# Four sums per SwiGLU on GpSimd instead of VectorE, in a two-layer decoder trunk on one core

## The chip, the cores and the metric

The kernel runs on one core of one Trainium2 chip. A core has TensorE (matrix products, called PE in the profile), VectorE (DVE), ScalarE (ACT), GpSimd (POOL) and SyncE (SP, which here only issues transfers). Each works through its own list of instructions in order, and they wait for each other by semaphores. The metric is the time of one execution in microseconds on the device; the profile is one such execution, recorded by the hardware profiler.

## The reference, cut to what matters

The input is one sequence of 512 tokens with 1024 features, all in float32. Two layers follow each other. Only the SwiGLUs matter here, of which there are four (two a layer):

```python
def swiglu(h, w_gate, w_up, w_down):
    return (jax.nn.silu(h @ w_gate) * (h @ w_up)) @ w_down

for l in range(DEPTH):                      # DEPTH = 2
    x = x + 0.5 * swiglu(rms_norm(x, ffn1_norm[l]), ffn1_wg[l], ffn1_wu[l], ffn1_wd[l])
    ...                                     # sliding-window attention and short convolution
    x = x + 0.5 * swiglu(rms_norm(x, ffn2_norm[l]), ffn2_wg[l], ffn2_wu[l], ffn2_wd[l])
return rms_norm(x, final_norm)
```

The hidden width of a SwiGLU is 2816, which is 22 blocks of 128.

## The kernel before, in words

Every float32 product is made of three faster products: each operand is split into a rounded "high" part (a cast on ScalarE, to `wh` for weights, `...h` for the stream) and the rest, a "low" part (a subtraction on VectorE, to `wl` or `...l`), and high x high, high x low and low x high are added up. The helper `split` (L225) records both. A few weights are split "far" (L229 to L231): ScalarE makes the high part and the negated copy, and a transfer issued by GpSimd adds the weight onto it in memory.

The SwiGLUs 1 to 4 are those of layer 0 (first, second) and layer 1 (first, second). Each begins with one "plain" pair of blocks (`plain`), its down projection (`down`), and then handles the other blocks in larger pairs (`winograd2`), with seven block products instead of eight. For it the stream (features x tokens, already normalized, tiles `hf`, L537) is cut into quarters b11, b12, b21, b22, and a weight of gate and up into a11, a12, a21, a22. From these come four sums of the stream, which are made once in each SwiGLU, for the first such pair, and serve all its pairs: t3 = b12 - b22 (L588), t2 = t3 - b11 (L589), t1 = b11 - b12 in the place of b12 (L591), t4 = t2 + b21 in the place of t2 (L593). Each is one instruction on 128 partitions x 1024 columns. t2 and t3 are made while the plain pair's down projection runs, t1 and t4 in the pair itself.

The products of a pair stand in the table `CHAINS`, in this order, with the weight that each uses: "x" a11 x b11; "w" a12 x b21; "x" s2 x t2; "y" s3 x t3; "x" s1 x t1; "y" a22 x t4; "x" s4 x b22. The s are sums of weights: the loads themselves add two tiles up (a second transfer onto the first, issued by GpSimd, L220), and VectorE adds others (L264, L284). Each product has two halves of the weight (12 matmuls of 512 columns each, 24 in all), and each half has its `wh` and `wl`. Weights are taken two splits ahead of their use, three buffers deep.

The order of the instructions of each engine is fixed when the program is built: a scheduler places each instruction by its own estimate of when its inputs are there. So a change of an instruction's engine moves others too. On the chip nothing overtakes on an engine.

The classes touched are `Norm`, which keeps one `Seven` for the stream's operands of a SwiGLU, and `Seven`, whose `make` builds an operand (the sum, if there is one, and then its split). `Seven` also serves the down projections (`shared`) and the mixer's output (`mix`); those are not touched.

Of the kernel before, what the change touches and what calls it, by code (L numbers as in the profile page):

```python
# [74 lines left out]
def trunk_kernel(  # L75
# [23 lines left out]
    nc = tc.nc  # L99
# [25 lines left out]
    def form(name, dt=F32R, shape=(P, KC // 2, H)):  # L125
        return xpool.tile(list(shape), dt, tag="xf", bufs=14, name=name)
# [97 lines left out]
    def split(hi, lo, raw, eng=nc.vector):  # L224
        return nc.scalar.copy(hi, raw), eng.tensor_sub(lo, raw, f32(hi))  # L225
# [210 lines left out]
    class Norm:  # L436
        def __init__(self, i):
            self.i = i
            self.h = [None] * KC
            self.acc = None  # L440
            self.inv = None
            self.full = []
            self.seven = Seven(self.full, room_g8, f"{i}")
            self.make, self.forms = self.seven.make, self.seven.forms
            self.pairs = {}
            self.begun = set()
            self.order = range(KC)
# [98 lines left out]
    class Seven:  # L546

        def __init__(self, full, room, name, far=()):  # L550

            self.full, self.room, self.name, self.forms = full, room, name, {}
            self.far = far

        def make(self, *names):
            for what in names:
                if what in self.forms:
                    continue
                full = self.full() if callable(self.full) else self.full
                b11, b12, b21, b22 = (  # L560
                    full[j][:, :, t * H : (t + 1) * H] if j < len(full) else None
                    for j in range(2)
                    for t in range(2)
                )
                kc = b11.shape[1]
                if kc == KC // 2:
                    hi, lo = (form(f"f{what}{n}_{self.name}") for n in "hl")
                else:
                    both = form(f"f{what}_{self.name}", shape=(P, 2, kc, H))
                    hi, lo = both[:, 0], both[:, 1]  # L570
                self.forms[what] = (hi, lo)
                if self.room is None:
                    if what == "t2":
                        nc.vector.tensor_sub(b12, b12, b22)
                        nc.vector.tensor_sub(b11, b12, b11)
                    if what == "t1":
                        nc.vector.scalar_tensor_tensor(
                            b12, b11, -1.0, b22, op0=ALU.mult, op1=ALU.subtract
                        )
                    if what == "t4":  # L580
                        nc.vector.tensor_add(b21, b11, b21)
                    places = {"b11": b11, "t2": b11, "t3": b12, "t1": b12, "b21": b21, "t4": b21, "b22": b22}
                    split(hi, lo, places[what])
                    continue
                if what == "t2":
                    self.sums = self.room(self.name)
                    t3, t2 = self.sums
                    nc.vector.tensor_sub(t3, b12, b22)  # L588
                    nc.vector.tensor_sub(t2, t3, b11)  # L589
                if what == "t1":  # L590
                    nc.vector.tensor_sub(b12, b11, b12)  # L591
                if what == "t4":
                    nc.vector.tensor_add(self.sums[1], self.sums[1], b21)  # L593
                src = {"b11": b11, "b21": b21, "b22": b22, "t1": b12}.get(what)
                if src is None:
                    src = self.sums[0 if what == "t3" else 1]
                (split_far if what in self.far else split)(hi, lo, src)
# [1129 lines left out]
```

## Time and profile before

| | |
|---|---|
| time, median of 3 runs | 1632.73 us (1632.26 to 1633.55) |
| the profiled execution | 1633.73 us, span from first to last instruction 1631.9 us |
| granted TensorE clock | 0.999 of full speed |
| TensorE busy | 1619.6 us, 99% of the span |
| VectorE busy | 1369.1 us, 84% |
| ScalarE busy | 1178.7 us, 72% |
| GpSimd busy | 223.5 us, 14% |
| the four sums on VectorE (L588, L589, L591, L593) | about 1.22 us each, 16 in all; in SwiGLU 1 from 44.7 us on, in SwiGLU 4 from 1327.1 us on |

In a timeline each row gives the start (us from the span's start), the length, the engine, the line and the operation, output<-inputs by the program's names, shapes, and how many instructions in a row were merged (x2); in brackets stands how long the engine was idle before and what ended that. In the chain of waits a row has start, length and what ran. A row of transfers says where they were issued, how many, their size and the median time from issue to landing. The length of a transfer's row in a timeline is that of its issue, not of its movement.

### The profile page before, as it was taken

What the parts mean: (1) busy time and instruction counts of PE and PEld (TensorE: products, weight loads), DVE (VectorE), ACT (ScalarE), POOL (GpSimd) and SP (SyncE); (2) the same over time, 40 slices, a digit from 0 to 9 for tenths busy, and PEclk for the clock granted to TensorE, in tenths of its full rate; (3) what the DMA queues carried; (4) which work ended last, traced back from release to release, by engine and by line L of the source; (5) the groups of instructions that cost most, each with busy time, mean ns of one, the idle gap of its engine ahead of it and who ended that gap; (6) DMA issues with size and microseconds to landing.
All of it is one profiled execution on the core that took longest, in us unless ns stands there. A gap on an engine that the chain in (4) does not pass through costs nothing.

```text
span 1631.9 us, 21170 instructions
## 1 busy us (share of the span) xinstructions
PE 1619.6 (99%) x7572; PEld 1348.3 (83%) x7572; DVE 1369.1 (84%) x1779; ACT 1178.7 (72%) x1510; POOL 223.5 (14%) x199
## 2 busy tenths in 40 slices
PE   9999999999999999999999999999999999999998
PEld 6788888888898888888888888888888988888887
DVE  7978798888899877797998777979788998677997
ACT  6667778867766577777865777788586767878665
POOL 1211111001121111111011111110012111111121
PEclk9999999999999999999999999999999999999999
DMA  9899989922497699999966999999136978999992
GB/s 271 194 230 221 215 203 234 251 65 74 125 240 176 175 218 218 214 209 240 229 154 173 227 214 221 199 246 228 52 91 156 227 153 213 222 222 229 230 264 70
DMA packets 307166, 318.12 MB, mean 195 GB/s; under 512 B 125612, under 2 KB 188660, under 8 KB 307060
## 3 DMA queue, kind: packets, MB, share of 16 engines
q1 hardware_dynamic: 265140, 230.63, 49.9%
q0 software_dynamic: 41200, 85.47, 30.9%
q8 instruction: 59, 0.97, 0.2%
q10 hardware_dynamic: 720, 0.66, 0.1%
q14 instruction: 47, 0.39, 0.1%
HBM read 264.29 MB, written 2.10 MB: 163 GB/s over the span
## 4 chain that ended last, share of the span: by engine, by line
PE 89%; DVE 5%; ACT 3%; DMA 1%; issue 1%; SPq 0%; ACTq 0%; DVEq 0%
PE x L823 26%; PE y L823 13%; PE x_s L823 8%; PE w L823 6%; PE acc L311 6%; PE acc L312 6%; PE acc L314 6%; PE y_s L823 5%; PE x_m L808 3%; PE w_s L823 2%; PE y_m L808 1%; DVE wl L225 1%; PE y_e L823 1%; PE acc L685 1%; PE x_e L823 1%
## 5 line engine op out<-in xcount | busy, mean ns | idle before, releaser
L225 DVE TENSOR_TENSOR wl<-raw,wh 128x1024 fp32r<-128x1024 f32 (+1 forms) x493 | 598.4, 1221 | 172.6 <-ACT wh L225 171.7
L225 ACT CAST wh<-raw 128x1024 fp32r<-128x1024 f32 (+1 forms) x493 | 513.1, 1045 | 296.1 <-PE x L823 95.0
L311 PE MATMUL acc<-xh,wh 128*128 128x512 f32 x392 | 153.1, 392 | 0.5 <-ACT wh L225 0.5
L312 PE MATMUL acc<-xl,wh 128*128 128x512 f32 x392 | 153.4, 391 | 0.0
L314 PE MATMUL acc<-xh,wl 128*128 128x512 f32 x384 | 149.8, 390 | 0.0
L220 POOL DMA_DIRECT2D raw<-in_ffn_wu_dram x40 | 50.2, 1263 | 384.6 <-DMA raw<-in_ffn_wu_dram 311.2
L311 PEld LDWEIGHTS acc<-xh,wh 128*128 128x128 f32 x392 | 73.8, 188 | 15.1 <-ACT wh L225 0.6
L312 PEld LDWEIGHTS acc<-xl,wh 128*128 128x128 f32 x392 | 73.7, 188 | 15.0 <-DVE xl L458 0.5
L314 PEld LDWEIGHTS acc<-xh,wl 128*128 128x128 f32 x384 | 72.2, 188 | 15.0
L220 POOL DMA_DIRECT2D raw<-in_ffn_wg_dram x40 | 48.4, 1232 | 201.9 <-DMA raw<-in_ffn_wu_dram 104.7
L220 POOL DMA_DIRECT2D raw<-in_ffn_wd_dram x34 | 41.1, 1218 | 254.5 <-DMA raw<-in_ffn_wd_dram 99.9
L264 DVE TENSOR_TENSOR raw<-raw,raw 128x1024 f32<-128x1024 f32 x58 | 70.5, 1219 | 6.2 <-DMA raw<-in_ffn_wu_dram 4.7
L1085 ACT COPY raw_a<-turned 128x1024 uint16<-128x1024 uint16 x48 | 63.5, 1355 | 0.0
L823 PE MATMUL x<-wl,ft2h 128*128 128x512 f32 x160 | 62.2, 390 | 1.1 <-DVE wl L225 1.1
L823 PE MATMUL w<-wl,fb21h 128*128 128x512 f32 x160 | 62.4, 390 | 0.6 <-DVE wl L225 0.6
L823 PE MATMUL y<-wh,ft4h 128*128 128x512 f32 x160 | 62.4, 390 | 0.1
L823 PE MATMUL w<-wh,fb21h 128*128 128x512 f32 x160 | 62.4, 390 | 0.0
L823 PE MATMUL y<-wh,ft3h 128*128 128x512 f32 x160 | 62.3, 390 | 0.0
L823 PE MATMUL x<-wh,ft2h 128*128 128x512 f32 x160 | 62.3, 389 | 0.0
L823 PE MATMUL x<-wh,ft1h 128*128 128x512 f32 x160 | 62.3, 389 | 0.0
L823 PE MATMUL x<-wh,ft2l 128*128 128x512 f32 x160 | 62.3, 389 | 0.0
L823 PE MATMUL w<-wh,fb21l 128*128 128x512 f32 x160 | 62.3, 389 | 0.0
(506 smaller groups left out, 4544.2 us busy)
## 6 DMA issues: line engine op xcount, KB each, us to landing
raw<-in_ffn_wu_dram SPq DMA_DIRECT2D x127, 512.0 KB, 5.6
raw<-in_ffn_wd_dram SPq DMA_DIRECT2D x105, 512.0 KB, 5.7
raw<-in_ffn_wg_dram SPq DMA_DIRECT2D x86, 512.0 KB, 5.5
raw<-in_ffn_wu_dram POOLq DMA_DIRECT2D x40, 512.0 KB, 9.1
raw<-in_ffn_wg_dram POOLq DMA_DIRECT2D x40, 512.0 KB, 6.3
raw<-in_w_in_dram SPq DMA_DIRECT2D x36, 512.0 KB, 4.1
raw<-in_ffn_wd_dram POOLq DMA_DIRECT2D x34, 512.0 KB, 9.8
raw<-raw POOLq DMA_DIRECT2D x21, 512.0 KB, 8.2
```

Of the source, the lines that this page charges most:

```text
L220: nc.gpsimd.dma_start(out=r, in_=rows_of(*more), accum_op=ALU.add)
L225: return nc.scalar.copy(hi, raw), eng.tensor_sub(lo, raw, f32(hi))
L264: nc.vector.tensor_add(a11, a11, s1)
L311: nc.tensor.matmul(acc, hi[:, k, :], rhs[k][0], start=k == first, stop=False)
L312: nc.tensor.matmul(acc, hi[:, k, :], rhs[k][1], start=False, stop=False)
L314: nc.tensor.matmul(acc, lo[:, k, :], rhs[k][0], start=False, stop=k == last)
L685: nc.tensor.matmul(opening[n], (lo if part == "w" else hi)[:, k, :], xl if part == "x" else xh, start=n not in begun, stop=k == KC - 1 and ...
L808: nc.tensor.matmul(accs[c // 2][:, c % 2, :], w[:, k, cols], x_[:, 2 * h + k, :], start=start and c % 2 == 0 and h + k + i == 0, stop=h + ...
L823: nc.tensor.matmul(accs[u], x_[:, 2 * h + k, tok], w[:, k, :], start=start and h + k + i == 0, stop=h + k == 2 and i == 2, skip_group_chec ...
L1085: nc.scalar.copy(words(raws[self.b][:, c, :]), self.to[:, :, c, :])
```

## The change

`Seven` gets the engine that makes the sums as an argument, VectorE by default; `Norm` passes GpSimd. The splits of the sums stay on ScalarE and VectorE.

```diff
-            self.seven = Seven(self.full, room_g8, f"{i}")
+            self.seven = Seven(self.full, room_g8, f"{i}", adder=nc.gpsimd)
...
-        def __init__(self, full, room, name, far=()):
+        def __init__(self, full, room, name, far=(), adder=nc.vector):
             self.full, self.room, self.name, self.forms = full, room, name, {}
+            self.adder = adder
...
                 if what == "t2":
                     self.sums = self.room(self.name)
                     t3, t2 = self.sums
-                    nc.vector.tensor_sub(t3, b12, b22)
-                    nc.vector.tensor_sub(t2, t3, b11)
+                    self.adder.tensor_sub(t3, b12, b22)
+                    self.adder.tensor_sub(t2, t3, b11)
                 if what == "t1":
-                    nc.vector.tensor_sub(b12, b11, b12)
+                    self.adder.tensor_sub(b12, b11, b12)
                 if what == "t4":
-                    nc.vector.tensor_add(self.sums[1], self.sums[1], b21)
+                    self.adder.tensor_add(self.sums[1], self.sums[1], b21)
```

In the built program this is the order on two of the engines (a weight's half in brackets; "transfer" is one issued by GpSimd):

```
ScalarE, SwiGLU 2 and 4
  before: ft2h, a11(2), ft3h, a12(1), a12(2), ... ft1h, s2(1), s2(2), ... ft4h
  after:  ft2h, ft3h, a11(2), ft1h, a12(1), ft4h, a12(2), ... s2(1), ... s2(2)
ScalarE, SwiGLU 3
  before: ft2h, a11(2), ft3h, a12(1), ft1h, a12(2), ... s2(1), s2(2), ft4h
  after:  ft2h, ft3h, ft1h, a11(2), a12(1), ft4h, a12(2), ... s2(1), ... s2(2)
ScalarE, SwiGLU 1
  before: a12(1), a12(2), ft2h, ... ft3h, ... ft1h, s2(1), s2(2), ... ft4h
  after:  a12(1), ft2h, a12(2), ft3h, ... ft1h, ... s2(1), ft4h, s2(2)

GpSimd after
  SwiGLU 1:    4 transfers of x, t3, 1 of x, t2, 3 of x, t1, t4
  SwiGLU 2, 4: t3, t2, far transfer of a11(1), 2 transfers of s3, t1, t4
  SwiGLU 3:    t3, t2, t1, far transfer of a11(1), 2 transfers of s3, t4
```

The low parts on VectorE follow in the same way: in SwiGLU 1 after: a12(1), ft2l, ft3l, a12(2), ft1l, s2(1), ft4l, s2(2); in SwiGLU 2 and 4 after: a12(1), ft1l, a weight sum, a12(2), a weight sum, s2(1), ft4l.

## The prediction, made before the changed kernel ran

> **What bounds the kernel now.** I read the page's busy line first, then a table of engine time over the four stretches in which a SwiGLU's first pair is computed, then the timelines of TensorE, GpSimd, ScalarE and VectorE and the chain of waits in those stretches.
>
> ```profile
> PE 1619.6 (99%) x7572; PEld 1348.3 (83%) x7572; DVE 1369.1 (84%) x1779; ACT 1178.7 (72%) x1510; POOL 223.5 (14%) x199
> ```
>
> TensorE is busy for 1619.6 of 1631.9 us. An idle GpSimd is no slack by itself: what counts is whether TensorE waits.
>
> ```profile
> 45.00:92.00 47.00, 45.25 (x198) 36.34 (x196) 41.70 (x42) 29.78 (x37) 8.89 (x9) 1.00 0.79 189
> 530.00:558.00 28.00, 28.00 (x125) 23.09 (x124) 26.94 (x28) 18.38 (x22) 1.21 (x1) 1.00 0.54 150
> 853.00:881.00 28.00, 28.00 (x125) 23.17 (x125) 25.85 (x27) 18.09 (x22) 1.84 (x2) 1.00 0.58 170
> 1334.00:1364.00 30.00, 30.00 (x142) 25.03 (x141) 27.02 (x28) 23.22 (x30) 2.90 (x3) 1.00 0.67 177
> ```
>
> The columns are the stretch, its length, then busy time of TensorE, weight load, VectorE, ScalarE and GpSimd. In SwiGLU 2, 3 and 4 TensorE has no idle time to win back. In SwiGLU 1 it idles 47.00 - 45.25 = 1.75 us. So the change can bring at most about 1.75 us, however much it relieves VectorE.
>
> **What is moved, and its price.** Sixteen instructions of VectorE (four in each of four SwiGLUs) go to GpSimd.
>
> ```profile
> 45.80 1.22 DVE L225 TENSOR_TENSOR fb21l<-hf,fb21h 128x1024 fp32r<-128x1024 f32 x1
> 46.93 1.22 DVE L589 TENSOR_TENSOR sums<-sums,hf 128x1024 f32<-128x1024 f32 x1
> ```
>
> Back to back they start 1.13 us apart, so VectorE is relieved of 16 x 1.13 = 18.1 us. No instruction of GpSimd in this trace has 1024 columns; the nearest is its product of 512 columns:
>
> ```profile
> 449.97 1.29 POOL L1658 TENSOR_TENSOR cc<-cc,inv 128x512 f32<-128x512 f32 x1
> ...
> 1601.91 3.52 POOL L1351 TENSOR_TENSOR ytok<-ytok,gain 128x512 f32<-128x512 f32 x2 [12.89 <-ACT ysq L1319]
> ```
>
> ```profile
> 1602.12 2.16 DVE L225 TENSOR_TENSOR wl<-raw,wh 128x1024 fp32r<-128x1024 f32 x1
> ...
> 1604.27 2.25 DVE L225 TENSOR_TENSOR fb22l_e<-raw_a,fb22h_e 128x1024 fp32r<-128x1024 f32 x1
> 1606.44 1.21 DVE L225 TENSOR_TENSOR wl<-raw,wh 128x1024 fp32r<-128x1024 f32 x1
> ```
>
> Alone it takes 1.29 us, so for twice the columns I take 2.6; the ends are 1.3 (the time doesn't grow) and 2 x 1.76 = 3.5 (each of the disturbed pair of 3.52), with a wait of up to 0.9 more. The second fence shows the disturbance: two GpSimd products (own time 2.58) and two VectorE subtractions (2 x 1.13) together fill 1601.91 to 1606.52, that is 4.6 us, the sum 4.84 and not the longer of the two. The engines took turns. So I add to each sum about 0.9 us of waiting wherever VectorE is busy (3.5 in all), and VectorE stands still for 2.6 us in each.
>
> The Trainium skill, page "SBUF — State Buffer", section "Who interferes with whom", says that a VectorE instruction with two SBUF inputs and a GpSimd instruction that reads SBUF exclude each other for their whole length. The trace agrees (4.6 against 4.84); by that rule the change takes up to 16 x 2.6 = 42 us of VectorE's time to save 18, where engines that ran side by side would make the first SwiGLU's loss below about 3 us smaller.
>
> **What is queued behind.** All engines work their queues in order. The built order puts ft1h and ft4h on ScalarE (they cast the third and fourth sum) ahead of casts of the a12 weights that TensorE needs sooner, and puts the sums on GpSimd between transfers. So weights wait for sums that nobody needs yet. One SwiGLU at a time:
>
> *Second SwiGLU.*
>
> ```profile
> 520.91 0.90 POOL L231 DMA_DIRECT2D wl<-raw  x1 [2.55 <-DVE a L225]
> 522.10 1.21 POOL L220 DMA_DIRECT2D raw<-in_ffn_wg_dram  x1 [0.29 <-issue]
> 533.35 1.21 POOL L220 DMA_DIRECT2D raw<-in_ffn_wg_dram  x1 [10.05 <-DMA raw<-in_ffn_wu_dram]
> ```
>
> ```profile
> 530.27 1.06 ACT L225 CAST wh<-raw 128x1024 fp32r<-128x1024 f32 x1 [2.32 <-issue]
> 532.99 1.06 ACT L225 CAST wh<-raw 128x1024 fp32r<-128x1024 f32 x1 [1.66 <-PE x L823]
> ...
> 536.60 1.06 ACT L225 CAST ft1h<-hf 128x1024 fp32r<-128x1024 f32 x1
> ```
>
> ```profile
> 530.41 5.44 PE x L823 x24
> 535.86 5.44 PE w L823 x24
> ```
>
> The two "wh" casts are the halves of a12, used by "w" (a12 x b21) from 535.86 and from 2.72 later. t1 now stands on GpSimd behind the transfer issued at 533.35, which waits for its tile to land: t1 runs 534.56 to 537.2, ft1h to 538.2, a12's first cast to 539.3, that is 3.4 late. Its low part comes 1.2 later on VectorE and is wanted 0.45 after the first product: 0.7 more. t4 ends at 537.2 + 3.5 = 540.7, ft4h at 541.8, the second cast at 542.8; its low part follows low part one, ft1l and a sum on VectorE, to 544, wanted at 535.86 + 4.1 + 2.72 + 0.45 = 543.1: about 0.9 more. **Second: 5.0.** The third far transfer (520.91) now goes out after t3 and t2, some 4 us later; I count that at nothing because it would still land near 531, where its product is due; where it doesn't, it is 1 to 2 us.
>
> *Fourth SwiGLU.* Same order, same steps.
>
> ```profile
> 1337.65 1.21 POOL L220 DMA_DIRECT2D raw<-in_ffn_wg_dram  x1 [9.91 <-DMA raw<-in_ffn_wu_dram]
> ```
>
> ```profile
> 1341.34 5.46 PE w L823 x24
> ```
>
> t1 1338.86 to 1341.5, ft1h 1342.5, cast 1343.6: 2.2 late, and the same 0.7 and 0.9. **Fourth: 3.8.**
>
> *Third SwiGLU.* Here three sums stand ahead of the third far transfer (the low part of the first a11 weight).
>
> ```profile
> 840.40 1.23 POOL L220 DMA_DIRECT2D raw<-in_ffn_wu_dram  x1
> 844.94 0.90 POOL L231 DMA_DIRECT2D wl<-raw  x1 [3.31 <-DVE sums L588]
> ...
> 857.26 1.21 POOL L220 DMA_DIRECT2D raw<-in_ffn_wg_dram  x1 [9.73 <-issue]
> ```
>
> ```profile
> 853.65 5.44 PE x L823 x24
> 859.09 5.44 PE w L823 x24
> ```
>
> ```profile
> wl<-raw POOLq DMA_DIRECT2D x10, 512.0 KB, 7.7
> raw<-in_w_out_dram POOLq DMA_DIRECT2D x8, 512.0 KB, 7.3
> x<-down POOLq DMA_DIRECT2D x8, 256.0 KB, 10.8
> ```
>
> The sums run from 841.6 for 3 x 2.6 and some 1.4 of waiting, to 850.8; the transfer goes out 5.9 us later than at 844.94. At the median of 7.7 us to land that is 858.5, wanted at 853.65 + 0.45: 4.4 late; if it lands faster for having left the crowd, less. I take 3.0. t4 behind the transfer of 857.26 ends near 861.7, ft4h and the second cast near 863.8, wanted near 864.8 after the delay: hidden behind the first wait. **Third: 3.0.**
>
> *First SwiGLU.*
>
> ```profile
> 41.54 6.67 POOL L1247 DMA_DIRECT2D x<-down  x7
> ```
>
> ```profile
> 48.15 1.05 ACT L225 CAST wh<-raw 128x1024 fp32r<-128x1024 f32 x1 [0.88 <-ACT wh L225]
> 49.11 1.05 ACT L225 CAST ft2h<-sums 128x1024 fp32r<-128x1024 f32 x1
> ```
>
> ```profile
> 50.85 0.39 PE L823 MATMUL w<-wh,fb21h 128*128 128x512 f32 x1
> ...
> 58.46 0.50 PE L823 MATMUL x<-wl,ft2h 128*128 128x512 f32 x1 [1.08 <-DVE wl L225]
> ```
>
> VectorE is full here. t3 stands behind four of the transfers (0.95 us each): 45.3 to 48.8; one transfer; t2 49.8 to 53.3; three transfers; t1 56.1 to 59.6; t4 to 63.1. a12's second cast (48.15 before) now follows ft2h: 53.3 + 2.1 = 55.4. Its low part follows ft2l and ft3l on VectorE, with t1 taking 2.6 in between: about 61.3, wanted at 50.85 + 2.72 + 0.45 = 54.0, 7.3 late. The s2 weight follows ft1h and ft1l: about 0.8 more. The 1.1 us that TensorE waited at 58.46 goes. **First: 7.0.**
>
> **The sum.** 7.0 + 5.0 + 3.0 + 3.8 = 18.8 us; TensorE never idles elsewhere enough to give it back. The profiled execution took 1633.73 (span 1631.9 and 1.8 around it), so 1652.5 there; it stood 1.0 above the median 1632.73, so **1651.5** for the median.
>
> **Rivals.** A difference under 0.2% (3.3 us) cannot be told from no change. *Relief wins (not slower):* the sums end before the casts behind them are wanted, and only the 1.75 us are won: 1631. It decides in the second SwiGLU: t1 would have to end by 533.7 (two casts before 535.86), before the transfer ahead of it was even issued at 533.35 + 1.21. For it speaks only that loads may land earlier once far transfers leave later. Chance 0.06 for anything up to 1636. *Short sums:* if a sum takes 1.3, first and third lose nothing, second 1.3 and fourth 1.3 less: about 5.0 - 1.3 + 3.8 - 1.3 = 6, 1639. Against it: 128x512 already takes 1.29. Chance 0.13. *The clock falls in the waits:*
>
> ```profile
> 1.19 2.74 PE L150 MATMUL idle<-zero 128*128 128x512 bf16 x6 [1.19 <-DVE warm L632]
> ...
> 4.08 1.03 PE L150 MATMUL idle<-zero 128*128 128x512 bf16 x2
> ```
>
> At the start a 512-column matmul comes every 0.43 us (the last ends later), later every 0.227 (5.44 / 24), and that lasts about 4 us, so it costs about 2 us. Should a wait bring that back, up to three waits of over 3 us add 6: 1658. No wait of over 1.1 us stands in the stretches above, so the trace can't say. Chance 0.11. The Trainium skill, "TensorE: Matmul & The Clock Gate", Part 1, states that an idle window of about 3.4 us halves the clock; my waits are about that long, and the window need not fall into them. *More blocking than counted* (sums of 4.4, the third far transfer at its 7.7): first 10, second 8, third 7, fourth 6: 1664. Chance 0.10. That the sums aren't moved is excluded: the built order has all 16 on GpSimd.
>
> **How the numbers follow.** The forecast has 0.60. From 1640 to 1664 it takes in the forecast's own spread, the clock, and half of the short and heavy cases each. Faster by over 0.2% would need 3.3 us where 1.75 are idle: 0.01. Within 0.2%: 0.05. Slower: 0.94.
>
> **What would show it.** Sums of 2.6 to 3.5 us on GpSimd at L588 to L593; TensorE waits of 3 to 4 us for ScalarE's wh at the "w" products of the second and fourth SwiGLU, ended by ft1h, and for VectorE's wl in the first; in the third a wait for the transfer of wl; VectorE instructions of over 2 us beside the sums. The prediction is wrong if TensorE stays full in the second stretch, if the sums take under 2 us, or if most of the loss stands outside the four stretches.

## The result, and the profile after

The changed kernel takes 1656.26 us (median of 4 runs, 1655.79 to 1660.96) against 1633.14 us of the kernel before on the same chip: a ratio of 1.0147, with a 95% interval of 1.0127 to 1.0167. The profiled execution took 1655.95 us, its span is 1653.7 us, and the mean granted TensorE clock is 0.995 (0.999 before). Line numbers from L552 on are higher by one than before: the sums stand at L589, L590, L592 and L594.

The busy line of the page:

```profile
PE 1626.6 (98%) x7572; PEld 1351.0 (82%) x7572; DVE 1377.7 (83%) x1763; ACT 1179.4 (71%) x1510; POOL 266.2 (16%) x215
```

VectorE has 16 instructions fewer, some 18 us of work, and yet is busy for 8.6 us longer. Where TensorE now waits (engine, product and line, what it waited for: us in total, times, longest):

```profile
PE w L824 <- DVE wl L225: 7.6, 5, 5.6
PE acc L330 <- DVE gate L950: 3.4, 2, 1.7
PE acc L333 <- DVE a L225: 2.9, 2, 1.4
...
PE w L824 <- DVE fb21l L225: 1.0, 1, 1.0
PE x L824 <- DMA wl<-raw: 1.0, 1, 1.0
```

No row waits for ScalarE's wh at a "w" product, which the prediction named for SwiGLU 2 and 4. What waits there are the products of the plain pair's down projection. SwiGLU 2, the timelines of GpSimd, VectorE and TensorE:

```profile
525.02 3.24 POOL L589 TENSOR_TENSOR sums<-hf,hf 128x1024 f32<-128x1024 f32 x1
528.35 3.24 POOL L590 TENSOR_TENSOR sums<-sums,hf 128x1024 f32<-128x1024 f32 x1
```

```profile
525.45 3.91 DVE L225 TENSOR_TENSOR fb11l<-hf,fb11h 128x1024 fp32r<-128x1024 f32 x1
529.28 0.68 DVE L950 TENSOR_TENSOR gate<-acc,gate 128x512 f32<-128x512 f32 x1
529.88 2.25 DVE L225 TENSOR_TENSOR a<-gate,a 128x512 fp32r<-128x512 f32 x1
```

```profile
530.01 0.50 PE L330 MATMUL acc<-a,wh 128*128 128x512 f32 x1 [1.67 <-DVE gate L950]
...
532.19 1.19 PE L333 MATMUL acc<-a,wh 128*128 128x512 f32 x4 [1.44 <-DVE a L225]
```

The low part fb11l begins 0.43 us after t3 and ends 1.1 us after it: it stood still for all of the rest of t3. "gate", which reads its accumulator from PSUM, runs beside t2 at its normal 0.68. Then "a", 0.68 long elsewhere, stands still until t2 ends. TensorE waits for each. SwiGLU 4 has the same waits, with something more:

```profile
1341.13 0.50 PE L330 MATMUL acc<-a,wh 128*128 128x512 f32 x1 [1.69 <-DVE gate L950]
...
1343.30 2.07 PE L333 MATMUL acc<-a,wh 128*128 128x512 f32 x4 [1.44 <-DVE a L225]
```

Here four products take 2.07 us instead of 1.19, and they come every 0.43 us until 1349, not every 0.227: the clock has fallen, and the mean granted clock of 1328 to 1375 is 0.93, against 1.00 around the equal waits of SwiGLU 2.

SwiGLU 1, VectorE and TensorE:

```profile
43.98 4.19 DVE L264 TENSOR_TENSOR raw<-raw,raw 128x1024 f32<-128x1024 f32 x1
48.10 3.41 DVE L225 TENSOR_TENSOR fb21l<-hf,fb21h 128x1024 fp32r<-128x1024 f32 x1
51.43 5.04 DVE L264 TENSOR_TENSOR raw<-raw,raw 128x1024 f32<-128x1024 f32 x1
...
59.80 3.39 DVE L225 TENSOR_TENSOR wl<-raw,wh 128x1024 fp32r<-128x1024 f32 x1
```

```profile
57.66 0.80 PE L824 MATMUL w<-wl,fb21h 128*128 128x512 f32 x1 [5.60 <-DVE wl L225]
```

These four take 3.4 to 5.0 us instead of 1.2. Two of them are sums of weights (L264) which the new built order puts ahead of the low part of a12's first half; before, they stood behind both halves (53.78 and 56.06). SwiGLU 3, GpSimd and TensorE:

```profile
852.24 4.23 POOL L589 TENSOR_TENSOR sums<-hf,hf 128x1024 f32<-128x1024 f32 x1
...
859.23 2.42 POOL L592 TENSOR_TENSOR hf<-hf 128x1024 f32<-128x1024 f32 x1
861.58 0.90 POOL L231 DMA_DIRECT2D wl<-raw  x1
```

```profile
866.21 0.50 PE L824 MATMUL x<-wl,fb11h 128*128 128x512 f32 x1 [0.97 <-DMA wl<-raw]
```

The sums on GpSimd take 2.42 to 4.23 us, waiting for VectorE included, and 3.16 in the mean of the 16. That of 859.23 took 2.42, and VectorE began nothing beside it in its first 1.1 us.

For each kernel below, this table gives how much later than in the trace of before TensorE's products run, stage by stage: the same groups of products are matched in the two traces, and a stage reaches from the plain pair's down projection into the second pair (up to 60 to 100 us later). All else, the plain pair's own products among it, is "elsewhere".

| kernel (profiled execution) | SwiGLU 1 | 2 | 3 | 4 | elsewhere | span against before |
|---|---|---|---|---|---|---|
| predicted | 7.0 | 5.0 | 3.0 | 3.8 | 0 | 18.8 |
| changed kernel | 7.4 | 3.7 | 2.8 | 7.8 | 0.1 | 21.8 |
| t23_gpsimd | 3.2 | 6.2 | 2.4 | 3.6 | 0.1 | 15.6 |
| t14_gpsimd | 2.7 | 5.4 | 6.6 | 4.4 | 0.2 | 19.3 |
| beside_sums | 10.4 | 10.0 | 7.5 | 11.4 | 4.7 | 44.0 |
| fill_waits | 9.9 | 9.1 | 2.6 | 10.6 | 2.9 | 35.1 |
| t14_late | 3.3 | 6.2 | 4.5 | 4.3 | 0.5 | 18.8 |
| all_late | 7.9 | 3.6 | 2.4 | 5.3 | -0.1 | 19.0 |
| held_sums | 8.5 | 14.5 | 14.1 | 17.5 | 3.8 | 58.4 |
| t4_transfer | -1.3 | 0.5 | 0.0 | 0.5 | 15.7 | 15.4 |
| t4_swiglu_only | -1.2 | 0.0 | 0.0 | 0.0 | 1.4 | 0.1 |
| fill_in_place | 7.8 | 9.2 | 2.6 | 11.5 | 2.6 | 33.7 |
| beside_copy | 6.3 | 2.6 | 1.7 | 2.5 | 0.6 | 13.8 |
| pieces_of_256 | 10.3 | 7.8 | 4.4 | 7.9 | 0.2 | 30.6 |

### The profile page after: what moved, and what is told of

Same layout as the page of the kernel before. It is cut to its first block, busy times and chain, and to the rows that moved or that the text cites. A ratio compares the mean times of both kernels' runs of the same rounds, so it can differ in the third digit from the quotient of the medians.

```text
span 1653.7 us, 21159 instructions
## 1 busy us (share of the span) xinstructions
PE 1626.6 (98%) x7572; PEld 1351.0 (82%) x7572; DVE 1377.7 (83%) x1763; ACT 1179.4 (71%) x1510; POOL 266.2 (16%) x215
## 4 chain that ended last, share of the span: by engine, by line
PE 80%; DVE 8%; ACT 4%; DMA 4%; issue 3%; SPq 0%; POOL 0%; ACTq 0%; DVEq 0%; POOLq 0%
PE x L824 25%; PE y L824 13%; PE x_s L824 7%; PE w L824 6%; PE acc L311 4%; PE acc L312 4%; PE acc L314 4%; PE y_s L824 4%; PE x_m L809 3%; PE w_s L824 3%; DVE wl L225 2%; PE y_m L809 1%; DMA raw<-in_ffn_wu_dram 1%; ACT wh L225 1%; PE x_e L824 1%
## 5 line engine op out<-in xcount | busy, mean ns | idle before, releaser
L225 DVE TENSOR_TENSOR wl<-raw,wh 128x1024 fp32r<-128x1024 f32 (+1 forms) x493 | 607.5, 1239 | 181.0 <-ACT wh L225 178.0
L264 DVE TENSOR_TENSOR raw<-raw,raw 128x1024 f32<-128x1024 f32 x58 | 77.6, 1337 | 3.8 <-issue 3.3
L824 PE MATMUL x<-wl,fb11h 128*128 128x512 f32 x160 | 62.4, 390 | 1.0 <-DMA wl<-raw 1.0
L824 PE MATMUL x<-wh,fb11l 128*128 128x512 f32 x160 | 62.3, 389 | 0.0
L824 PE MATMUL y<-wh,ft3l 128*128 128x512 f32 x160 | 62.2, 389 | 0.0
```

The costliest lines, as they stand in the source:

```text
L264: nc.vector.tensor_add(a11, a11, s1)
L824: nc.tensor.matmul(accs[u], x_[:, 2 * h + k, tok], w[:, k, :], start=start and h + k + i == 0, stop=h + k == 2 and i == 2, skip_group_chec ...
```

## The experiments

Theory A is that GpSimd's sums stop VectorE's subtractions, theory B that the new order of the queues makes weights wait for sums.

### Which sums cost: two of the four on GpSimd

```diff
 t23_gpsimd: t3, t2 on self.adder (GpSimd); t1, t4 back on nc.vector
 t14_gpsimd: t1, t4 on self.adder (GpSimd); t3, t2 back on nc.vector
```

> Only the first two sums (t3 and t2) are made by GpSimd; t1 and t4 go back to VectorE. The changed kernel's trace has its delays at 7.6 us (SwiGLU 1), 4.15 (2), 2.8 (3) and 6.5 (4), 21.8 in all. Theory A (GpSimd's sums stop VectorE's subtractions, and TensorE waits for whichever subtraction is stopped): the waits of the second and fourth SwiGLU, for 'gate' and 'a' in the down projection, come from t3 and t2 alone and stay whole: about 4 and 4 to 6.5. SwiGLU 1 loses only t1's and t4's share (low part of a12, stopped by t4): 3 to 6. SwiGLU 3's far transfer goes out earlier by t1's length: 0 to 1.5. Sum 11 to 18, so 1644 to 1651. Theory B (the order of the queues, the prediction's: casts of t1 and t4 ahead of a12's): with t1 and t4 on VectorE, SwiGLU 2 and 4 lose nothing (0 to 1 each), and most of what is left stands in SwiGLU 1: 1636 to 1641.

> Only t1 and t4 are made by GpSimd; t3 and t2 go back to VectorE. Theory A (stopped subtractions): nothing stands beside the plain pair's subtractions in SwiGLU 2 and 4 any more, so the waits for 'gate' and 'a' are gone there; what is left is what t1 and t4 stop themselves, at most one sum's length each: 0 to 2.5 in each of SwiGLU 2, 3 and 4. SwiGLU 1: 2 to 5. Sum 3 to 9: 1636 to 1642. Theory B (the order of the queues): the casts of t1 and t4 still stand ahead of a12's, and nothing upstream hides them now: TensorE waits 2.5 to 4 us for ScalarE's wh at the 'w' products of SwiGLU 2 and 4, so 5.0 and 3.8, with 2 to 3 in SwiGLU 3 and 3 to 5 in SwiGLU 1: 1647 to 1650.

Measured: 1651.58 us (ratio 1.0107, 1.0092 to 1.0122), just above theory A's range, and 1653.55 us (1.0117, 1.0102 to 1.0132), above theory B's. Each half of the change costs nearly as much as the whole: 15.6 and 19.3 us in the traces, 34.9 together, against 21.8. With t3 and t2 alone the waits in the down projections are all there, as theory A says, with one more for "a" in SwiGLU 3:

```profile
PE acc L333 <- DVE a L225: 5.0, 3, 2.1
PE acc L330 <- DVE gate L950: 3.3, 2, 1.7
```

With t1 and t4 alone they are gone, and the waits of theory B, those of the prediction, stand in their place (waits of TensorE, then ScalarE and TensorE in SwiGLU 2):

```profile
PE w L824 <- ACT wh L225: 7.9, 3, 3.4
```

```profile
538.37 1.04 ACT L225 CAST ft1h<-hf 128x1024 fp32r<-128x1024 f32 x1 [8.71 <-POOL hf L592]
539.32 1.99 ACT L225 CAST wh<-raw 128x1024 fp32r<-128x1024 f32 x2
```

```profile
540.41 0.67 PE L824 MATMUL w<-wh,fb21h 128*128 128x512 f32 x1 [2.84 <-ACT wh L225]
```

ScalarE waited 8.71 us for t1 with both casts of a12 behind it. So both theories hold, and in the changed kernel the second cost is hidden. Two things hide it there. TensorE comes to these products 3.7 us later, by the wait in the down projection. And t1 comes sooner, which the prediction had thought unlikely: GpSimd's transfer ahead of t1 waits for a load of 512 KB issued by SyncE (`raw<-in_ffn_wu_dram`), and this load lands sooner. These are its row of transfers with t1 and t4 alone, its row in the changed kernel, and there the transfer that waits for it and a12's first cast:

```profile
raw<-in_ffn_wu_dram SPq DMA_DIRECT2D x1, 512.0 KB, 9.5
```

```profile
raw<-in_ffn_wu_dram SPq DMA_DIRECT2D x1, 512.0 KB, 4.4
```

```profile
535.64 1.20 POOL L220 DMA_DIRECT2D raw<-in_ffn_wg_dram  x1 [1.98 <-DMA raw<-in_ffn_wu_dram]
```

```profile
541.39 1.06 ACT L225 CAST wh<-raw 128x1024 fp32r<-128x1024 f32 x1 [1.03 <-PE acc L312]
```

In the changed kernel t3 and t2 hold back GpSimd's far transfer (to 531.52) and the one after it, and the load goes out ahead of them, at 530.55. In SwiGLU 2 and 4 of the traces here the load takes 8.3 to 10.0 us where it goes out 1.8 us or more behind the far transfer, and 3.7 to 5.0 where it goes out 0.7 us or more ahead of it. TensorE reaches the down projection 5.8 us later in the changed kernel than with t1 and t4 alone (526.80 against 521.05), but t1 starts only 0.9 later (536.40 against 535.48). The cast of a12 then waits for TensorE (its acc) and not for t1, and it is done at 542.45, 4.4 us ahead of the first "w" product (546.81). The 4.8 us that t1 gained and the 3.7 of the earlier wait are each more than the 2.84 that TensorE waited for wh; no run separates them. Theory A's numbers for this run (3 to 9) and theory B's for the other failed.

### The order mended

The casts ft1h and ft4h are queued behind those of the weights taken last (`state["cast"]` is the last such cast). In t14_late t3 and t2 are on VectorE as well.

```diff
-                (split_far if what in self.far else split)(hi, lo, src)
+                late = what in ("t1", "t4") and self.adder is nc.gpsimd
+                with tc.issue_after(state["cast"]) if late else nullcontext():
+                    (split_far if what in self.far else split)(hi, lo, src)
```

> As in the run with only t1 and t4 on GpSimd, but their casts ft1h and ft4h (ScalarE) are queued behind the casts of the weights taken last (both halves of a12, and of s2), as in the kernel before. That run lost 19 us, with TensorE waiting 2.84, 3.42 and 1.63 us for ScalarE's wh at the first 'w' product of SwiGLU 2, 3 and 4. Theory B (the order of the queues): these three waits and the 2 to 3 us that follow each are gone: 1634 to 1639. Theory A (GpSimd's sums stop VectorE, and that alone costs): nothing changes, 1650 to 1654.

> The changed kernel (all four sums on GpSimd), with the casts ft1h and ft4h queued behind a12's and s2's. Theory A (stopped subtractions of the plain pair) says that the waits in SwiGLU 2 and 4 for 'gate' and 'a' (1.7 and 1.4 us) come first and hide what the order would cost there: within 3 us of the changed kernel, 1653 to 1658. Theory B (order alone): 5.0 and 3.8 us are won in SwiGLU 2 and 4: 1645 to 1649.

Measured: t14_late 1656.07 us (1.0140, 1.0126 to 1.0154), all_late 1654.33 us (1.0144, 1.0127 to 1.0161). For all_late theory A's forecast came out: SwiGLU 2 loses 3.6 as before, the load landing early there too (4.6 us). For t14_late neither theory had the whole: the three waits for wh are gone, and the time is no better. GpSimd and VectorE in SwiGLU 2:

```profile
536.71 2.88 POOL L592 TENSOR_TENSOR hf<-hf 128x1024 f32<-128x1024 f32 x1
539.07 2.85 POOL L594 TENSOR_TENSOR sums<-sums,hf 128x1024 f32<-128x1024 f32 x1
```

```profile
535.61 7.40 DVE L225 TENSOR_TENSOR wl<-raw,wh 128x1024 fp32r<-128x1024 f32 x2
```

Two low parts, which take 1.13 + 1.22 = 2.35 us undisturbed, fill 7.40, because t1 and t4 run back to back beside the second: 5.05 us of standing still. Where t1 no longer holds a12's casts, it holds a12's low part.

### GpSimd's instructions without any dependence

VectorE makes all sums as before; GpSimd works beside it on a spare tile for nobody, in the same places (the code is shown in part).

```diff
                     nc.vector.tensor_sub(t3, b12, b22)
                     nc.vector.tensor_sub(t2, t3, b11)
+                    self.beside(b21, b22, 2)
...
+        def beside(self, p, q, n=1):
+            if self.adder is nc.gpsimd:
+                for _ in range(n):
+                    nc.gpsimd.tensor_sub(spare, p, q)     # beside_copy: tensor_copy(spare, p)
```

> VectorE makes all four sums as in the kernel before, and GpSimd computes four differences of the same size (128x1024, two inputs in float32, written as bfloat16 to a spare tile) in each SwiGLU at the places where the sums stand in its list; nobody waits for these. So VectorE is not relieved, and no cast or subtraction depends on GpSimd. Theory A (stopped VectorE): VectorE's subtractions beside them take 2.2 to 4.2 us as in the changed kernel, and TensorE waits: 3 to 5 us in SwiGLU 2 and 4 each, 3 to 8 in SwiGLU 1, which has VectorE's own 4.5 us of sums besides, 1 to 3 in SwiGLU 3: 1643 to 1656. Theory B (queue order) and the theory that GpSimd's sums are only late in the chain of what depends on them: almost nothing is lost, except the far transfer behind the differences in SwiGLU 3 (up to 3): 1632 to 1636, with VectorE's instructions at 1.22 us throughout.

> As the run beside_sums (VectorE makes all sums; GpSimd's instructions are waited for by nobody), but GpSimd copies 1024 columns (one input) instead of taking a difference of two inputs. Theory A1 (any instruction of GpSimd that reads memory holds VectorE's two-input subtractions off): VectorE's subtractions beside the copies are longer than 1.22 us by about the length of a copy, and the loss is the copies' length by that of the differences (2.4), some 15 to 43 us: 1650 to 1677. Theory A2 (only two-input instructions of GpSimd do it): VectorE's subtractions stay at 1.22, and the time is 1632 to 1638.

Measured: beside_sums 1677.20 us (1.0261, 1.0242 to 1.0280), above theory A's 1643 to 1656; beside_copy 1647.52 us (1.0089, 1.0076 to 1.0102), a little below A1's 1650 and clear of A2's 1638. The busy lines of the two pages:

```profile
PE 1637.0 (98%) x7572; PEld 1353.2 (81%) x7572; DVE 1409.6 (84%) x1779; ACT 1178.5 (70%) x1510; POOL 267.6 (16%) x215
```

```profile
PE 1626.3 (99%) x7572; PEld 1351.3 (82%) x7572; DVE 1383.4 (84%) x1779; ACT 1178.9 (72%) x1510; POOL 247.7 (15%) x215
```

The same 1779 instructions of VectorE take 1409.6 - 1369.1 = 40.5 us longer beside 16 differences, 2.5 us each, which is a difference's own length (2.42 at 859.23 above); and 14.3 us longer beside 16 copies, 0.9 each, of 1.38 us that the shortest copy takes. This is the direct evidence for theory A: results that nobody waits for, and about the whole length of each difference lost to VectorE. One input instead of two doesn't lift it; less is lost. The Trainium skill, page "SBUF — State Buffer", section "Who interferes with whom", says that a VectorE instruction with two SBUF inputs contends with any GpSimd instruction that reads SBUF; both runs agree, and so does "gate" above, whose accumulator comes from PSUM and which kept its 0.68 beside t2.

### The sums held back, and cut in pieces

```diff
 held_sums (with the late casts of all_late): t3 behind the plain pair's last low part
+                        behind = nc.gpsimd.tensor_copy(mark, f32(state["low"])).ins
+                    with tc.issue_after(behind) if behind else nullcontext():
                         self.adder.tensor_sub(t3, b12, b22)
 pieces_of_256 (with the order of the changed kernel)
+                    for k in cut:                         # four slices of 256 columns
-                    self.adder.tensor_sub(t3, b12, b22)
+                        self.adder.tensor_sub(t3[:, k], b12[:, k], b22[:, k])
```

> All four sums on GpSimd, the casts queued late as in the run all_late, and t3 held on GpSimd behind an instruction of one column that reads the last low part of the plain pair ('a'), so that t3 and t2 no longer run beside the subtractions that the down projection waits for. Both causes together (stopped subtractions and order): the waits for 'gate' and 'a' in SwiGLU 2 and 4 are gone, and 0 to 2 us each are left there; SwiGLU 1 keeps 5 to 8 and SwiGLU 3, where the far transfer stands behind even later sums, 2 to 5: 1642 to 1650. Rival (GpSimd's sums are simply late for what depends on them): later sums cost more, 1657 to 1665, with TensorE waiting at the s2 x t2 products.

> The changed kernel with each of GpSimd's sums cut into four instructions of 256 columns. If the engines take turns instruction by instruction, VectorE gets in after a piece of about 0.6 us: fb11l and a beside the sums take 1.2 to 2.0 us instead of 3.9 and 2.25, the waits for gate and a in SwiGLU 2 and 4 shrink to 0 to 1 us, SwiGLU 1 loses 3 to 6: 1638 to 1650. Rival (GpSimd keeps its turn through all four pieces, or the pieces' own start costs more than it frees): 1654 to 1662, with VectorE's instructions as long as in the changed kernel.

Measured: held_sums 1691.12 us (1.0355, 1.0341 to 1.0369), a miss. In SwiGLU 2 "a" is back at 0.68 and the waits in the down projection are gone, but GpSimd's list shows what came instead:

```profile
544.08 1.21 POOL L220 DMA_DIRECT2D raw<-in_ffn_wg_dram  x1 [9.59 <-DMA raw<-in_ffn_wu_dram]
...
544.96 2.87 POOL L594 TENSOR_TENSOR sums<-hf,hf 128x1024 f32<-128x1024 f32 x1
```

The sums have slipped behind a transfer that adds a weight onto another and waits 9.59 us for that to land; in the changed kernel t3 and t2 went ahead of it. It is dearer than the rival's 1665 too, and what was late was GpSimd's queue, not its arithmetic: TensorE waits 10.65 us at the first "w" product (558.49), not at s2 x t2. With t3 and t2 out of its way the far transfer goes out ahead of the load again (532.35 against 534.68), and the load takes 8.7 us. pieces_of_256 took 1663.50 us (1.0187, 1.0174 to 1.0200), on the rival's side and a little above its 1662. In SwiGLU 2 one subtraction of VectorE stood still through nearly all of the eight pieces of t3 and t2 (GpSimd, VectorE, TensorE):

```profile
527.57 3.67 POOL L591 TENSOR_TENSOR sums<-hf,hf 128x256 f32<-128x256 f32 x4
530.37 4.55 POOL L593 TENSOR_TENSOR sums<-sums,hf 128x256 f32<-128x256 f32 x4
```

```profile
528.04 6.32 DVE L225 TENSOR_TENSOR fb11l<-hf,fb11h 128x1024 fp32r<-128x1024 f32 x1
```

```profile
535.02 0.80 PE L330 MATMUL acc<-a,wh 128*128 128x512 f32 x1 [4.08 <-DVE gate L955]
```

In SwiGLU 1, pieces and VectorE's instructions did alternate (four in a row of 1.74 to 1.76 us from 45.63 on). What decides between the two is open.

### The waits filled, to test the clock

```diff
+    def fill(acc, n):                # adds products of zeros to a sum
+        for _ in range(n):
+            nc.tensor.matmul(acc, zero[:, :P], zero, start=False, stop=False)
 fill_waits:    24 ahead of the first w<-wl in SwiGLU 1;
                7 and 6 in the second half (k = 1) of the down projection's first block, SwiGLU 2 and 4
 fill_in_place: 7 and 6 in its first half (k = 0), where TensorE waits; none in SwiGLU 1
```

> The changed kernel, with products of zeros added on TensorE (added to the sums of the waiting products, so that the result is unchanged) just ahead of the places where it waited: 24 matmuls of 512 columns (24 x 0.227 = 5.4 us) ahead of the first w<-wl in SwiGLU 1 (it waited 5.60 there), 7 (1.6 us) and 6 (1.4 us) ahead of the two waits in the down projections of SwiGLU 2 and 4 (1.67 and 1.44). They are as long as the waits, so they cost nothing by themselves if VectorE's times stay. Theory A with the clock (the 11 and about 13 matmuls at 0.427 behind the waits of SwiGLU 1 and 4 are TensorE's clock, lowered for having stood still): behind the filled waits matmuls come every 0.227 us, SwiGLU 1 wins 2.2 to 2.5, SwiGLU 4 2.5 to 3, SwiGLU 2 nothing: 1650 to 1652. Rival (the slow matmuls have another cause, such as memory that is busy, and would come with or without a wait): they stay, and the time is 1655 to 1658.

> The changed kernel with products of zeros (result unchanged) at the places of the two waits in the down projection of SwiGLU 2 and 4: 7 ahead of the first product of the fourth column block (wait of 1.67), 6 ahead of the first product with the low part of 'a' (1.44). The run fill_waits had them behind these waits, not in them. Clock theory: standing still there lowers TensorE's clock somewhat later (13 matmuls at 0.43 us in SwiGLU 4 of the changed kernel, 12 in SwiGLU 2 of the run with t2 and t3 alone), and with the waits filled no matmuls of 0.43 us stand behind them in either: SwiGLU 4 loses 3.5 to 4.5 instead of 6.5, SwiGLU 2 still 4: 1653 to 1655. Rival (slow stretches come with or without a wait): slow stretches in at least one of the two, 1656 to 1660.

Measured: 1667.72 us (1.0206, 1.0191 to 1.0222) and 1665.26 us (1.0194, 1.0180 to 1.0209): both times miss. In fill_waits the 7 and 6 came after the waits instead of in them, and the first 24 products of the down projection, the zeros not counted, lost 8.2 us in each of SwiGLU 2 and 4. In both kernels the added products moved VectorE's order too (a weight sum slipped ahead, beside t1 and t4), so the totals say nothing of the clock. What follows the waits does. TensorE in SwiGLU 1 of fill_waits:

```profile
53.36 5.13 PE L326 MATMUL w<-zero 128*128 128x512 bf16 x23
58.89 0.50 PE L832 MATMUL w<-wl,fb21h 128*128 128x512 f32 x1 [0.40 <-DVE wl L225]
59.23 0.40 PE L832 MATMUL w<-wh,fb21h 128*128 128x512 f32 x1
...
64.46 0.77 PE L832 MATMUL w<-wl,fb21h 128*128 128x512 f32 x1 [2.52 <-DVE wl L225]
65.03 0.63 PE L832 MATMUL w<-wh,fb21h 128*128 128x512 f32 x1
```

Behind the filled wait products come every 0.23 us; behind the next, unfilled wait of 2.52 they come every 0.43. But the 2.4 us of slow products of the changed kernel were not won: TensorE came sooner to a second low part that was no sooner there. In SwiGLU 1 VectorE sets the end, and the clock cost nothing of its own. In SwiGLU 4 of fill_in_place:

```profile
1347.48 1.69 PE L326 MATMUL acc<-zero 128*128 128x512 bf16 x7
...
1349.87 1.47 PE L326 MATMUL acc<-zero 128*128 128x512 bf16 x6
1351.49 1.20 PE L340 MATMUL acc<-a,wh 128*128 128x512 f32 x4
```

No slow product follows. Over the first 24 products of the down projection, the zeros not counted, the changed kernel lost 3.66 us in SwiGLU 2 and 6.46 in SwiGLU 4; fill_in_place loses 3.70 and 3.69. So the fallen clock cost 2.8 us in SwiGLU 4. In t23_gpsimd, whose waits are the same, it fell in SwiGLU 2 (6.31) and not in SwiGLU 4 (3.67); in beside_sums in both.

Why one pair of waits brings the fall and an equal pair doesn't stands in the record of the granted clock. In each of the 14 traces all its changes lie a whole number of steps of 3.41 us apart: in the changed kernel half clock stands from 55.69 to 62.51 and from 1342.51 to 1349.34, two steps each, with 375 steps between them. Where the steps begin differs from trace to trace. Engine time in such steps, two around the waits of SwiGLU 2 and two around those of SwiGLU 4 in the changed kernel (columns as in the prediction; the granted clock is the third number from the end):

```profile
526.73:530.14 3.41, 1.74 (x9) 1.11 (x8) 3.41 (x3) 1.21 (x2) 3.33 (x2) 1.00 1.08 213
530.14:533.56 3.42, 1.98 (x8) 1.34 (x9) 3.42 (x3) 3.36 (x4) 3.42 (x3) 1.00 0.99 219
1339.10:1342.51 3.41, 1.07 (x4) 0.30 (x2) 3.41 (x3) 1.48 (x3) 3.33 (x2) 1.00 1.07 192
1342.51:1345.92 3.41, 2.62 (x6) 2.14 (x7) 3.41 (x4) 2.16 (x3) 2.28 (x3) 0.50 0.99 243
```

In SwiGLU 2 each wait fell into a step of its own, with TensorE idle for 1.67 and 1.44 us, and the clock stayed. In SwiGLU 4 one step holds 2.34 us of idle time, and the next is at half clock. Counted over all 14 traces, each of the 30 steps at full clock with more than 1.77 us idle is followed by half clock, none of the 6621 with 1.5 or less is, and the 17 in between go either way. So the slow products come with the waits, and an idle time of about half a step is enough where it falls into one step.

### A sum off VectorE without arithmetic on GpSimd

From the kernel before: a transfer adds b21 onto t2. The code is shown in part; t4_transfer does it for all streams that share the SwiGLUs' buffers, t4_swiglu_only for the four SwiGLUs alone.

```diff
-                    nc.vector.tensor_add(self.sums[1], self.sums[1], b21)
+                    nc.gpsimd.dma_start(out=self.sums[1], in_=b21, accum_op=ALU.add)
...
+                if step == 3:
+                    norm.make("t4")      # its cast and subtraction, two products later
```

> The kernel before, with t4 alone moved off VectorE, and not to GpSimd's arithmetic: a transfer adds b21 onto t2 in memory (GpSimd only issues it), and t4's cast and subtraction are queued two products later. VectorE is relieved of one instruction of 1.13 us in each SwiGLU and nothing reads memory on GpSimd. If it is the sharing of memory by GpSimd's arithmetic that costs, this costs nothing: 1631 to 1635, and at most the 1.08 us that TensorE waits in SwiGLU 1 is won. Rival (the place in GpSimd's list and the wait for a result that comes late cost as much as the sum): 1637 to 1645.

> As the run t4_transfer (t4 added up by a transfer, VectorE relieved, no arithmetic on GpSimd), but in the four SwiGLUs alone: in that run the mixer's operand t4 went the same way, and 9 of its 15 us stand there (TensorE waited for ft1l_m and wh in the mixers), none in SwiGLU 3. If moving a sum off VectorE is harmless as long as GpSimd does no arithmetic, and the loss was the mixer's: 1631 to 1634 (at most the 1.75 us that TensorE idles in SwiGLU 1 can be won). Rival (the later place of t4's cast and subtraction costs in each SwiGLU): 1636 to 1645.

Measured: t4_transfer 1649.16 us (1.0103, 1.0089 to 1.0117), a miss of the expectation: the edit also reached the mixer's operands, and 15.7 us stand outside the stages of the table, in the mixers and from there to the first product of the down projections behind them:

```profile
PE x_m L819 <- DMA ft1l_m<-m: 3.7, 2, 2.5
PE x_m L819 <- ACT wh L225: 3.5, 4, 1.0
PE acc L330 <- ACT a L225: 2.9, 2, 1.5
```

Kept to the SwiGLUs it takes 1633.40 us against 1632.86 (1.0007, 0.9995 to 1.0018): no change. SwiGLU 1 wins 1.2 us and gives it back later; the other three lose nothing. So moving this one sum, with its cast queued later, is harmless when GpSimd does no arithmetic for it, and as TensorE was full there was nothing more to win. The other three were not tried in this way.

## Why the prediction was right, and where it was not

Sign and size were right (1651.5 forecast, 1640 to 1664; 1656.26 measured), and its first mechanism was: a sum takes 2.42 us without disturbance (2.6 forecast) and VectorE stands still for that long. The sum of 18.8 is nearer to 21.8 than its terms deserve: in all four SwiGLUs most of the loss stands at another product than forecast, so that much of the size is luck.

- **What the change may win.** At most 1.75 us, the forecast said. The waits at ft2's products went, as it said, and t4_swiglu_only won 1.2 us in SwiGLU 1, for a while.
- **Second SwiGLU (5.0, measured 3.7).** The step that failed is "weights wait for sums that nobody needs yet", as the place of the loss. The step is real (t14_gpsimd, 2.84 us at that product), but in the changed kernel it costs nothing. What costs is an earlier wait: t3 and t2 stand beside fb11l and "a" of the plain pair, which the prediction counted at nothing because it looked for blocked subtractions only behind the sums it was following. It had listed VectorE standing still for 2.6 us in each sum; it did not walk through who was beside t3 and t2. It also took t1's start from the trace of before, as if the load ahead of it would land as late as there. That load landed in 4.4 us instead of 8.8, and t1 ended at 539.28, which is 531.8 once the 7.5 us are taken off by which TensorE came late to this SwiGLU. So the condition that the prediction set for its rival "relief wins" (t1 done by 533.7) was met, for the reason that it named (loads land earlier once far transfers leave later), and the SwiGLU still lost.
- **Fourth SwiGLU (3.8, measured 7.8).** The same step failed in the same way: 3.7 us in the down projection. To this come 2.8 of the fallen clock and 1.3 at a later pair: a transfer that adds onto a weight, issued at 1383.40, took 15.8 us to land (10.8 before), a weight sum (L264) began only then, at 1399.23, and TensorE waited 1.04 us at 1402 for the low part behind it. Why it landed late is open. The rival of the clock, put at 2 us a wait, was thus right in kind, and cost once, not three times.
- **Third SwiGLU (3.0, measured 2.8).** The mechanism is there, but it makes up less than half; that the size fits is luck. The far transfer went out at 861.58, 5.5 us later once the delay of 11.1 up to there is taken off (5.9 forecast), but it landed in 4.6 us rather than the median of 7.7, so TensorE waited 0.97 us for it and lost 1.2. Another 1.3 went at the two halves of a12 in the "w" products (waits of 0.25 and 0.40 for VectorE's wl), which the prediction counted at nothing, and the rest later.
- **First SwiGLU (7.0, measured 7.4).** Right in size, engine and kind (VectorE's wl at the "w" products), wrong in place: not the second but the first half of a12 (5.60), and fb21l (1.01). The prediction followed the casts and low parts of the new order and missed that the two weight sums of L264 had moved ahead of them, where t3 and t1 stopped them.
- **Relief wins, short sums, more blocking.** A sum of 1.3 is excluded (2.42). Blocking of 4.4 a sum did not come: two sums took over 4 us (4.07 and 4.23), but their mean is 3.16. The third far transfer at its 7.7 did not come either.

The causes don't add up. All four sums cost 21.8 us, two of them 15.6 and the other two 19.3; with the order mended the latter two cost 18.8, by another wait. A wait that is taken away here uncovers the next one, and a sum that is moved also moves transfers, which changes when loads land.

## What to carry to other kernels

Before an elementwise instruction goes to an idle GpSimd, list what VectorE has to do beside it: its subtractions with two inputs in SBUF stop for the whole length, so here 18 us of relief came with some 27 us of standing still (8.6 + 18.1), and who waits for each of them matters more than who waits for the sum. When several waits come from one cause, price the first in time, then walk the rest of the timeline again with it in place, loads and transfers included; don't add them up as terms of a sum. A transfer that adds in memory moved one of the sums (t4) without loss, where its result wasn't needed soon.

## What the runs showed of the hardware that was not expected

- A one-input copy on GpSimd stops VectorE's two-input subtractions too: 2.05 us and more instead of 1.22, 14.3 us in 16 copies.
- A load of 512 KB took 3.7 to 5.0 us where it went out ahead of GpSimd's far transfer and 8.3 to 10.0 us where it went out behind it. An engine that is late to issue a transfer can so bring another transfer in sooner.
- Cutting a sum into pieces doesn't let VectorE in reliably: beside eight pieces a subtraction took 6.32 us, while elsewhere the engines alternated piece by piece.
- TensorE's clock fell after much shorter waits than the 5.60 us of SwiGLU 1: after a single wait of 2.52 us in fill_waits and of 1.86 us in beside_copy (seven products at 0.43 each), and after 1.67 and 1.44 us in some executions and not in others, at 2.8 us a time in SwiGLU 4 of the changed kernel. What counted was the idle time within one step of a 3.41 us grid: over 1.77 us always brought half clock, 1.5 or less never. The Trainium skill, page "TensorE: Matmul & The Clock Gate", Part 1, speaks of an idle window of about 3.4 us that is free-running. The steps of 3.41 us, which begin elsewhere in each trace, agree; but the window need not be idle throughout, since about half of it was enough here.
